# Latent convolution on 32x32 tiles of the array, and layer norm with the channels on the partitions

## The chip, the cores and the metric

The kernel runs on one core of one Trainium2 chip, with the engines TensorE (PE, its weight loads PEld), VectorE (DVE), ScalarE (ACT) and GpSimd (POOL), and with all its transfers issued from SyncE (SP). The metric is the time of one execution on the device in microseconds (us), the median of several runs.

## The reference

One layer with two branches runs over 256 context tokens and 2048 latent tokens (32 rows of 64 columns) of 1024 channels. Cut to what the change touches:

```python
u = (rms_norm(x, g_pre) * (1 + scale) + shift) @ w_in      # -> z, xbc, dt, ga, gb, gsil
y_ssd = rms_norm(ssd_scan_both_ways(...) * silu(z), norm_g)
h = ga * sigmoid(gb)                            # conformer branch, 1024 channels
h = depthwise_conv(h, conv_w, conv_b)           # 31 taps along axis 1 of the grid
h = silu(layer_norm(h, ln_g, ln_b)) * silu(gsil)  # norm over the 1024 channels of a token
out = concat([y_ssd, h]) @ w_out                # (tokens, 2048) @ (2048, 1024)
y = x + gate * rms_norm(out, g_post)
```

For the latent tokens the grid is 32 x 64 and the convolution runs along its 32 rows, so each channel's convolution is a 32x32 banded matrix applied to a 32x64 image.

## The kernel before

The tokens are 18 tiles of 128 (`NT`; two of them context). The projections come first, with float32 split into a high and a low float32r part, so that each product is three matmuls (`mm_cm`, L378 to L380; in the profile `sp`, `xp`, `ga`, `gb` are their PSUM banks). The scan over the tiles (`py`, `po`, `pst`) and the convolutions are woven between them as `extra`, step by step. Last comes the **out stage**, a loop over `order` (the tiles from 17 down to 2, then 1 and 0), from about 1420 us to the end.

The program's order is not only the written one: the tile framework is told to schedule with its own timeline, and it settles in which order each engine takes its instructions. Each engine then works strictly in that order, and waits at an instruction whose inputs are late.

**Latent convolution** (`lat_conv`, eight groups `j` of 128 channels). Channels lie in four row blocks of 32 partitions (a partition is a grid row). Each step `u` of four expands 32 channels' bands from `kd` into a block-diagonal 128x128 operand `kbuf` (four ACT copies a step, L622; two buffers), and eight matmuls (L634, `cp`) take 64 columns of image `x` as stationary operand and `kbuf` as the moving one, with the two 64-column halves of the array. VectorE adds the bias and puts the result into `vt` (L639), and it is stored by token into `CVL`. `ctx_conv` does the context's convolution on VectorE, transposes it (L594) and stores it by token into `CVC`.

**Layer norm and out stage.** For every tile:
- `conf_pre` (L1037): load `cn` by token, statistics with `bn_stats`, `cr` = rstd on GpSimd (`rstd_of`, L135), and `(n - mean) * rstd` in one VectorE pass (L1047).
- `conf_act` (L1050): eight transposes (L1058, `ct`) put channels on the partitions, ScalarE applies `silu` with the channel's scale and bias (L1061) from PSUM, VectorE multiplies with `gsl` (L1063). `conf_hl` splits into `ph` and `pl`.
- `ssd_pre` (L968): `qo` matmuls, `y` of the scan times silu(z), its square, summed over eight blocks (`zr`, L991).
- `ssd_norm` (L1002): one matmul sums `zr` over the partitions (`pm`, L1004), then `yms` and `yr` = rstd. `ssd_scale` (L1010): one matmul spreads `yr` over the partitions (L1012), VectorE scales `y` (L1013); `ssd_hl` splits it into `yh` (ACT, L1019) and `yl` (VectorE, L1020).
- `out_part` (L1073): 96 matmuls of 512 columns (L1078, `op`), 48 with the tile's `yh`/`yl` and 48 with its `ph`/`pl`, into two PSUM banks.
- `finish` (L1081): sums of squares of the two banks on ScalarE (L1087), then scale, add and store.

Of the kernel before, what the change touches and what calls it, by code (L numbers as in the profile page):

```python
# [67 lines left out]
def backbone_kernel(ctx, tc, xa, xt_in, cols, rows, wconv, conf_b, gp_row, bg_row, state0, w_mod, w_dt, w_in, w_out,  # L68
# [19 lines left out]
    CVC = dram("cvc", [NCTX * P, D])  # L88
    CVL = dram("cvl", [LAT, D])
# [437 lines left out]

    def gab_unit(half, j, hb):
        wb = next_w()
        wa = next_w()  # L530
# [72 lines left out]
    def lat_conv(j, lp, kbuf):  # L603
        cbb = lp.tile([P, HD], F32, tag="cbb", name=f"cbb{j}", bufs=2)
        for h in range(2):
            c0 = j * P + h * 64
            DMA.dma_start(cbb[h * 64:(h + 1) * 64], conf_b[c0:c0 + 64].partition_broadcast(64))
        kd = lp.tile([P, 32, 32], F32, tag="kd", name=f"kd{j}", bufs=1)
        for c4 in range(4):
            src = bass.AP(tensor=wconv.tensor, offset=(j * 4 + c4) * 64 * 32, ap=[[32, 32], [1, 1024]])  # L610
# [4 lines left out]
        for c4 in range(4):
            DMA.dma_start(x[c4 * 32:(c4 + 1) * 32], src[c4])

        def expand(u):
            kt = kbuf[u % 2]
            for c4 in range(4):  # L620
                rs = slice(c4 * 32, (c4 + 1) * 32)
                S.copy(kt[rs, :, rs].rearrange("p (h q) r -> p h q r", h=2),  # L622
                       kd[rs].rearrange("p r (h u q) -> p u h q r", h=2, u=4)[:, u])

        vt = lp.tile([P, 32, HD], F32, tag="cvv", name=f"cvv{j}", bufs=1)
        yield
        expand(0)
        yield
        for u in range(4):
            kt = kbuf[u % 2]  # L630
            ps = bank("ss", f"cp{j}_{u}")
            for q in range(4):
                for h in range(2):
                    T.matmul(ps[h * 64:(h + 1) * 64, q * P:(q + 1) * P], x[:, h * 16 + u * 4 + q, :], kt[:, h * 4 + q, :],  # L634
                             start=True, stop=True)
# [3 lines left out]
            V.scalar_tensor_tensor(vt[:, ::-1, u * 16:(u + 1) * 16].rearrange("p r c -> p c r"),  # L639
                                   ps.rearrange("p (c r) -> p c r", r=32), 0.5,  # L640
                                   cbb[:, u * 16:(u + 1) * 16].unsqueeze(2).to_broadcast([P, 16, 32]), MUL, ADD)
# [288 lines left out]
    for u in range(2):  # L930
        G.memset(kbuf[u], 0.0)
# [105 lines left out]
    def conf_pre(i):  # L1037
# [3 lines left out]
        for h in range(2):  # L1041
            V.bn_stats(bs[:, 6 * h:6 * h + 6], n[:, h * 512:(h + 1) * 512])
# [187 lines left out]
```

## Time and profile before

| | |
|---|---|
| median of 3 runs | 1878.53 us (1878.14 to 1878.75) |
| the profiled execution | 1882.2 us, span 1880.5 us |
| mean granted TensorE clock | 0.986 |
| latent stage, 950 to 1360 us | PE busy 392.55 us of 410, clock 0.98 |
| out stage, 1420 to 1880 us | PE busy 449.88 us of 460, clock 0.99 |

The table's execution is the one profiled; the runs of the first line were not profiled. Matmuls are pipelined: the duration of one includes the time until its result has landed, and what it takes of the array is read from the start of the next. In rows of the timeline the columns are start, duration, engine, line, operation, output and inputs, count, and in brackets the idle time ahead of the group and what ended it. In rows by line they are busy time, mean ns of one, idle time before them. `PEclk` is the granted clock as a share of full speed.

### The profile page before, as it was taken

The page shows a single profiled execution, that of the slowest core. Times are in us where ns is not written, and L with a number is a line of the kernel's source. Part 1 is how long each engine was busy: PE and PEld are TensorE (multiplying, and loading weights), DVE is VectorE, ACT ScalarE, POOL GpSimd, SP SyncE. Part 2 cuts the span into 40 slices and gives each one's busy share as a digit, 9 for nine tenths or more (in the row PEclk, how much of TensorE's full clock was granted, in tenths as well). Part 3 has the DMA queues.
Part 4 walks back from the last instruction along what each step waited for, and adds up shares of the span by engine and source line. Part 5 has one row for each costly group of instructions (what it writes and reads, how often), then busy time and mean ns, then how long its engine had stood idle before and what let it go on. Part 6 is the DMA issues. An engine that isn't in the chain of part 4 may idle for free.

```text
span 1880.5 us, 26833 instructions
## 1 busy us (share of the span) xinstructions
PE 1825.6 (97%) x9739; PEld 1504.6 (80%) x9739; DVE 1188.2 (63%) x1699; ACT 839.5 (45%) x1786; POOL 269.0 (14%) x351
## 2 busy tenths in 40 slices
PE   7899999999999999999999899999999999999998
PEld 4788887787887888888877677777887888888887
DVE  2477887776545553577585768655427676766662
ACT  3646424443455441644355666675414232232321
POOL 0002001111111100100001011110013333333220
PEclk9899999999999999999999999999999999999999
DMA  8556575564677754545587897978887655555532
GB/s 302 212 200 198 211 239 179 176 222 155 211 269 225 225 200 169 165 154 188 179 195 215 210 242 194 278 185 234 239 268 239 191 174 173 165 172 173 175 102 78
DMA packets 290400, 375.29 MB, mean 200 GB/s; under 512 B 85206, under 2 KB 187478, under 8 KB 290268
## 3 DMA queue, kind: packets, MB, share of 16 engines
q1 hardware_dynamic: 290268, 373.58, 64.2%
q8 instruction: 77, 1.26, 0.3%
q14 instruction: 55, 0.45, 0.1%
HBM read 243.92 MB, written 129.59 MB: 199 GB/s over the span
## 4 chain that ended last, share of the span: by engine, by line
PE 62%; DMA 5%; ACT 3%; issue 3%; DVE 2%; SPq 2%; POOL 0%; POOLq 0%; DVEq 0%; ACTq 0%
PE op L1078 20%; PE sp L378 6%; PE sp L379 6%; PE sp L380 6%; DMA lb<-lt 3%; PE xp L379 2%; PE xp L378 2%; PE xp L380 2%; PE py L720 2%; PE ga L378 2%; PE ga L380 1%; PE po L727 1%; PE ga L379 1%; PE qo L985 1%; PE gb L378 1%
## 5 line engine op out<-in xcount | busy, mean ns | idle before, releaser
L684 ACT ACTIVATE lb<-lb,WB 128x128 f32<-128x128 f32 x576 | 184.1, 391 | 150.9 <-POOL lb L676 149.0
L378 PE MATMUL sp<-hh,wh 128*128 128x512 f32 (+1 forms) x640 | 239.7, 375 | 2.6 <-DVE sth L550 2.6
L379 PE MATMUL sp<-hl,wh 128*128 128x512 f32 (+1 forms) x640 | 237.0, 370 | 0.0
L380 PE MATMUL sp<-hh,wl 128*128 128x512 f32 (+1 forms) x640 | 236.7, 370 | 0.2 <-DMA wl<-wld 0.2
L676 POOL TENSOR_SCALAR_AFFINE_SELECT lb<-lb 128x512 f32<-128x512 f32 x144 | 108.7, 760 | 749.7 <-ACT el L673 416.1
L378 PE MATMUL xp<-hh,wh 128*128 128x512 f32 (+1 forms) x480 | 179.1, 375 | 6.1 <-ACT wh L353 4.0
L379 PE MATMUL xp<-hl,wh 128*128 128x512 f32 (+1 forms) x480 | 179.1, 373 | 0.2 <-DVE hl L299 0.2
L380 PE MATMUL xp<-hh,wl 128*128 128x512 f32 (+1 forms) x480 | 179.2, 374 | 0.0
L475 DVE SCALAR_TENSOR_TENSOR cva<-raw,cwh,cva 128x1280 f32<-128x1280 f32 (+1 forms) x96 | 142.7, 1495 | 15.5 <-ACT cva L469 13.6
L378 PEld LDWEIGHTS sp<-hh,wh 128*128 128x128 f32 x640 | 121.0, 189 | 24.3 <-DVE sth L550 3.1
L380 PEld LDWEIGHTS sp<-hh,wl 128*128 128x128 f32 x640 | 121.0, 189 | 21.6 <-DMA wl<-wld 0.7
L379 PEld LDWEIGHTS sp<-hl,wh 128*128 128x128 f32 x640 | 121.2, 189 | 20.1 <-issue 0.5
L378 PE MATMUL gb<-hh,wh 128*128 128x512 f32 (+1 forms) x320 | 121.9, 381 | 3.4 <-DVE gth L539 3.4
L378 PE MATMUL ga<-hh,wh 128*128 128x512 f32 (+1 forms) x320 | 120.4, 376 | 2.6 <-ACT gth L536 2.6
L379 PE MATMUL gb<-hl,wh 128*128 128x512 f32 (+1 forms) x320 | 119.3, 373 | 0.0
L380 PE MATMUL gb<-hh,wl 128*128 128x512 f32 (+1 forms) x320 | 119.1, 372 | 0.0
L380 PE MATMUL ga<-hh,wl 128*128 128x512 f32 (+1 forms) x320 | 118.1, 369 | 0.0
L379 PE MATMUL ga<-hl,wh 128*128 128x512 f32 (+1 forms) x320 | 117.9, 369 | 0.0
L590 DVE SCALAR_TENSOR_TENSOR cg<-cg,cv 128x256 f32<-128x256 f32 x240 | 113.3, 497 | 2.5
L550 DVE SCALAR_TENSOR_TENSOR sth<-sth,sp 128x512 f32<-128x512 f32 (+1 forms) x80 | 50.4, 630 | 98.4 <-ACT sth L549 98.4
L378 PEld LDWEIGHTS xp<-hh,wh 128*128 128x128 f32 x480 | 92.0, 192 | 23.0 <-ACT wh L353 4.8
L688 DVE TENSOR_TENSOR lb<-lb,lb 128x512 f32<-128x512 f32 x72 | 51.6, 717 | 85.6 <-ACT lb L684 55.8
(219 smaller groups left out, 3860.8 us busy)
## 6 DMA issues: line engine op xcount, KB each, us to landing
lb<-lt SPq DMA_DIRECT2D x144, 256.0 KB, 4.2
wr<-in_w_in SPq DMA_DIRECT2D x88, 256.0 KB, 4.9
whd<-wh SPq DMA_DIRECT2D x44, 512.0 KB, 3.4
wld<-wl SPq DMA_DIRECT2D x44, 512.0 KB, 4.7
wh<-whd SPq DMA_DIRECT2D x44, 512.0 KB, 5.2
wl<-wld SPq DMA_DIRECT2D x44, 512.0 KB, 5.6
xT<-xb SPq DMA_DIRECT2D x18, 512.0 KB, 5.4
yp<-yg SPq DMA_DIRECT2D x36, 256.0 KB, 4.5
```

Source lines behind the costliest of these rows:

```text
L378: T.matmul(ps[:, :BN], wh[:, k, :], hh[:, k, :], start=(k == 0), stop=False)
L379: T.matmul(ps[:, :BN], wh[:, k, :], hl[:, k, :], start=False, stop=False)
L380: T.matmul(ps[:, :BN], wl[:, k, :], hh[:, k, :], start=False, stop=(k == KT - 1))
L475: V.scalar_tensor_tensor(a[:, :n], raw[:, t:t + n], cwh[:, ct * 5 + t:ct * 5 + t + 1], a[:, :n], MUL, ADD)
L550: V.scalar_tensor_tensor(th, th, 1.0, ps[:, :BN], ADD, MUL)
L590: V.scalar_tensor_tensor(acc, g[:, t:t + 256], cv[:, w0 + t:w0 + t + 1], acc, MUL, ADD)
L676: G.affine_select(E[g, hq, d], E[g, hq, d], pattern=[[0, 4], [sg, P]], compare_op=ALU.is_ge, fill=NEG, base=0, channel_multiplier=-sg)
L684: S.activation(lb[:, h, :], lb[:, h, :], AF.Exp, bias=WB[:, i, c + h:c + h + 1])
L688: V.tensor_tensor(a, a, E[g, hq, 1], ADD)
L720: T.matmul(py[g][j * HD:(j + 1) * HD, q * P:(q + 1) * P], xt[g][:, h * HD:(h + 1) * HD], E[g, hq, 0][:, t, :], start=True, stop=True)
L727: T.matmul(po[g][:, q * P:(q + 1) * P], Sf[g][:, q * P:(q + 1) * P], bc[:, 2 + g, :], start=True, stop=True)
L1078: T.matmul(pso[n], lhs[:, k % 8, :], w[:, n * 512:(n + 1) * 512], start=(k == 0 and m == 0), stop=(k == 15 and m == 2))
```

## The change

**Latent convolution.** Each 32x32 band matrix stays as it is (`kt`, one ACT copy of 128x1024 for a group) and becomes the stationary operand of one 32x32 tile of the array; a channel's 32x64 image is the moving one. A group's 128 channels are dealt out so that channel 32u+4q+a lies in row block a and goes to column block u: 64 matmuls fill two banks, in two runs. The result has channels, not tokens, in order, and is stored by channel into one array `CV`. `ctx_conv` drops its transposes and stores there too. The next group's `kd` and `cx` are loaded one group ahead, if `gab_unit` has stored them (`gl_done`, not shown); the bias is loaded once.

**Layer norm.** A tile of `CV` is loaded with channels on the partitions, so the eight transposes go. The mean over the channels is a sum of eight blocks on VectorE (`sum8`) and one matmul with `ones` (`cm`, L1062), and is subtracted from a tile two ahead (`conf_mean`). Its square (ACT, L1068) and its sum `nq` follow one tile ahead (`conf_square`), and its rstd goes through the same two small matmuls as that of the scan's norm: `norms` (`pm`, two columns, L1018) and `spread` (`pn`, two blocks of one bank, L1029). `zr` is summed with `sum8` too. `cn` has two buffers, `v` still one. `silu` reads SBUF.

```diff
-    CVC = dram("cvc", [NCTX * P, D])
-    CVL = dram("cvl", [LAT, D])
+    CV = dram("cv", [D, NT * P])
...
+        S.mul(o, acc, 0.5)
+        DMA.dma_start(CV[j * P:(j + 1) * P, 0:256], o)
...
+        kd = lp.tile([P, 32, 32], F32, tag="kd", name=f"kd{j}", bufs=2)
+        x = lp.tile([P, 32, 64], F32, tag="cx", name=f"cx{j}", bufs=2)
+        lat_in[j] = kd, x
+        for a in range(4):
+            rs = slice(a * 32, (a + 1) * 32)
+            src = bass.AP(tensor=wconv.tensor, offset=(j * 4 + a) * 64 * 32, ap=[[32, 32], [1, 1024]])
+            DMA.dma_start(kd[rs].rearrange("p r g -> p (r g)"), src)
+            DMA.dma_start(x[rs], GL[j][:, 256:].rearrange("(g a) (r w) -> a r g w", a=4, w=64)[a])
+
+    def lat_conv(j, lp, cbb, more):
+        if j not in lat_in:
+            lat_load(j, lp)
+        kd, x = lat_in.pop(j)
+        yield
+        kt = lp.tile([P, 32, 32], F32, tag="kt", name=f"kt{j}", bufs=1)
+        S.copy(kt[:, :, ::-1].rearrange("p g r -> p r g"), kd)
+        if more(j + 1):
+            lat_load(j + 1, lp)
...
+        vt = lp.tile([P, 32, 64], F32, tag="cvv", name=f"cvv{j}", bufs=1)
         for h in range(2):
...
+            ps = {a: bank("ss", f"cp{j}_{a}") for a in (2 * h, 2 * h + 1)}
+            for q in range(8):
+                for u in range(4):
+                    for a in ps:
+                        rs = slice(a * 32, (a + 1) * 32)
+                        T.matmul(ps[a][u * 32:(u + 1) * 32, q * 64:(q + 1) * 64], kt[rs, u * 8 + q, :], x[rs, u * 8 + q, :],
+                                 start=True, stop=True)
+            yield
+            for a in ps:
+                V.scalar_tensor_tensor(vt[:, a::4, :], ps[a].rearrange("p (c w) -> p c w", w=64), 0.5,
+                                       cbb[:, j, a::4].unsqueeze(2).to_broadcast([P, 8, 64]), MUL, ADD)
+            yield
...
         for u in range(4):
...
+            c0 = j * P + u * 32
+            DMA.dma_start(CV[c0:c0 + 32, 256:].rearrange("c (r w) -> r c w", w=64), vt[u * 32:(u + 1) * 32])
...
+
+    def sum8(out, t, v):
+
+        V.tensor_tensor(t, v[:, 0:4, :], v[:, 4:8, :], ADD)
+        V.tensor_tensor(t[:, 0:2, :], t[:, 0:2, :], t[:, 2:4, :], ADD)
+        V.tensor_tensor(out, t[:, 0, :], t[:, 1, :], ADD)
+        return out
...
-        zr = p1.tile([P, P], F32, tag="zr", name=f"zr{i}", bufs=2)
-        V.tensor_reduce(zr, z.rearrange("p q l -> p l q"), mybir.AxisListType.X, ADD)
+        zr = sum8(p1.tile([P, P], F32, tag="zr", name=f"zr{i}", bufs=2), z[:, 0:4, :], z)
...
+    rows8 = lambda t: t.unsqueeze(1).to_broadcast([P, 8, P])
...
+    def norms(i, yz, nq):
+
         pm = bank("ss", f"pm{i}")
...
+        src = [(c, e, t[1]) for c, e, t in ((0, 4.0 * EPS, yz), (1, EPS, nq)) if t]
+        for c, e, t in src:
+            T.matmul(pm[:, c:c + 1], t, ones[:, 0:1], start=True, stop=True)
+        rs = []
+        for c, e, t in src:
+            ms = p1.tile([P, 1], F32, tag=f"ms{c}", name=f"yms{i}{c}", bufs=2)
+            V.tensor_scalar(ms, pm[:, c:c + 1], 1.0 / D, e, MUL, ADD)
+            rs.append((c, rstd_of(p1, ms, f"yr{i}{c}")))
+        return rs
+
+    def spread(i, rs):
+        pb = bank("ss", f"pn{i}")
+        for c, r in rs:
+            T.matmul(pb[:, c * P:(c + 1) * P], r.to_broadcast([P, P]), ident, start=True, stop=True)
+        return pb
...
+    def conf_load(i):
+        n = p2.tile([P, 8, P], F32, tag="cn", name=f"cn{i}", bufs=2)
+        DMA.dma_start(n, CV[:, i * P:(i + 1) * P].rearrange("(c p) t -> p c t", p=P))
         return n
 
-    def conf_act(i, n):
+    def conf_mean(i, n):
+        t = p2.tile([P, 4, P], F32, tag="cs", name=f"cs{i}", bufs=1)
+        t = sum8(t[:, 0, :], t, n)
+        mean = bank("ss", f"cm{i}")[:, 0:P]
+        T.matmul(mean, ones, t, start=True, stop=True)
+        V.scalar_tensor_tensor(n, rows8(mean), -1.0 / D, n, MUL, ADD)
+        return n
...
+    def conf_square(i, n):
+        v = p2.tile([P, 8, P], F32, tag="v", name=f"v{i}", bufs=1)
+        S.activation(v, n, AF.Square)
+        return v, sum8(p2.tile([P, P], F32, tag="nq", name=f"nq{i}", bufs=2), v[:, 0:4, :], v)
+
+    def conf_act(i, n, v, pb):
...
+        V.tensor_tensor(n, n, rows8(pb[:, P:2 * P]), MUL)
+        for k in range(8):
+            S.activation(v[:, k, :], n[:, k, :], AF.Silu, bias=cv[:, C_LNB + k:C_LNB + k + 1],
+                         scale=cv[:, C_LNG + k:C_LNG + k + 1])
...
     for a, i in enumerate(order):
         last = a + 1 == NT
         nxt = None if last else order[a + 1]
         pt = conf_hl(i, v)
         banks(i)
-        out_part(pso[i], yh, 0, 1)
         if not last:
-            yr = ssd_norm(nxt, yz)
-        out_part(pso[i], yh, 1, 3)
+            v, nq = conf_square(nxt, n)
+        out_part(pso[i], yh, 0, 2)
+        if not last:
+            rs = norms(nxt, yz, (v, nq))
+        y = yz[0]
         if a + 2 < NT:
+            n2 = conf_load(order[a + 2])
             yz = ssd_pre(order[a + 2], order[a + 2] == NCTX - 1)
+        out_part(pso[i], yh, 2, 6)
         if not last:
-            n = conf_pre(nxt)
-        out_part(pso[i], yh, 3, 6)
+            pb = spread(nxt, rs)
+            yhn = ssd_scale(nxt, y, pb)
+        out_part(pso[i], yh, 6, 8)
+        out_part(pso[i], pt, 8, 9)
         if not last:
-            yhn = ssd_scale(nxt, yr)
-        out_part(pso[i], yh, 6, 8)
-        out_part(pso[i], pt, 8, 10)
+            v = conf_act(nxt, n, v, pb)
+        out_part(pso[i], pt, 9, 11)
+        if a + 2 < NT:
+            n = conf_mean(order[a + 2], n2)
         if last:
-            out_part(pso[i], pt, 10, 16, (0,))
-            out_part(pso[i], pt, 10, 16, (1,))
+            out_part(pso[i], pt, 11, 16, (0,))
+            out_part(pso[i], pt, 11, 16, (1,))
         else:
-            v = conf_act(nxt, n)
-            out_part(pso[i], pt, 10, 16)
+            out_part(pso[i], pt, 11, 16)
             yh = yhn
         if i == 1:
```

How this moves instructions on TensorE and VectorE (rows of after carry the line numbers of the changed kernel, as do the lines named in this section). First TensorE in the latent stage, at the first group's first run. Before, eight matmuls (`cp_0` is the bank of step 0) stand between the projection's; `ga` is a bank of the projection:

```order
4287 L379 MATMUL ga_1_4_8687<-hl_7344,wh_1_8346 128x512
4288 L380 MATMUL ga_1_4_8687<-hh_7343,wl_1_8345 128x512
4289 L634 MATMUL cp_0_8691<-kbuf_8337,cx_8634 64x128 x8
4290 L378 MATMUL ga_1_4_8687<-hh_7343,wh_1_8346 128x512
4291 L379 MATMUL ga_1_4_8687<-hl_7344,wh_1_8346 128x512
```

After, the run begins so, and goes on in pairs for 64 matmuls:

```order
4283 L378 MATMUL ga_1_4_8669<-hl_7331,wh_1_8334 128x512
4284 L379 MATMUL ga_1_4_8669<-hh_7330,wl_1_8333 128x512
4285 L634 MATMUL cp_0_8674<-cx_8615,kt_8630 32x64
4286 L634 MATMUL cp_1_8675<-cx_8615,kt_8630 32x64
4287 L634 MATMUL cp_0_8674<-cx_8615,kt_8630 32x64
4288 L634 MATMUL cp_1_8675<-cx_8615,kt_8630 32x64
```

There are 16 such runs where there were 30 with `kbuf`.

TensorE in the out stage. Before, the spread of the scan's norm (`pm<-ident,yr`) for the next tile stands inside the running tile's matmuls with `yh` and `yl`; `op_0` and `op_1` are the tile's banks, `woh` and `wol` the weights' parts:

```order
6442 L1078 MATMUL op_0_14110<-woh_12574,yl_14007 128x512
6443 L1078 MATMUL op_1_14111<-woh_12574,yl_14007 128x512
6444 L1012 MATMUL pm_14118<-ident,yr_14122 128x128
6445 L1078 MATMUL op_0_14110<-woh_12683,yh_14006 128x512
6446 L1078 MATMUL op_1_14111<-woh_12683,yh_14006 128x512
```

24 more with `y` and 36 with `ph` and `pl` follow it before the next tile's first `op` (60 in all). After, the same spread is the first `pn` of a pair, with the mean's `cm` between them. In one tile (`op_0_14763` runs, `op_0_14959` comes next):

```order
7474 L1029 MATMUL pn_14854<-ident,yr_14788 128x128
7475 L1062 MATMUL cm_14908<-cs_14904,ones 128x128
7476 L1029 MATMUL pn_14854<-ident,yr_14792 128x128
7477 L1093 MATMUL op_0_14763<-woh_13729,pl_14760 128x512
7478 L1093 MATMUL op_1_14764<-woh_13729,pl_14760 128x512
7479 L1093 MATMUL op_0_14959<-woh_13065,yh_14858 128x512
7480 L1093 MATMUL op_1_14960<-woh_13065,yh_14858 128x512
7481 L1093 MATMUL op_0_14959<-wol_13064,yh_14858 128x512
7482 L1093 MATMUL op_1_14960<-wol_13064,yh_14858 128x512
7483 L1018 MATMUL pm_14979<-ones,zr_14822 128x1
7484 L992 MATMUL qo_15003<-ct_14992,Sb_13062 128x128 x4
7485 L992 MATMUL qo_15009<-ct_14992,Sb_13063 128x128 x4
```

Two matmuls with `pl` of the running tile follow the pair, then four with the next tile's `yh`, and only then `pm` and `qo`. In the tile ahead of it eight follow, and `pm` and `qo` come before the first with `yh`:

```order
7367 L1029 MATMUL pn_14658<-ident,yr_14596 128x128
7368 L1093 MATMUL op_0_14567<-woh_13723,pl_14564 128x512
7369 L1093 MATMUL op_1_14568<-woh_13723,pl_14564 128x512
7370 L1093 MATMUL op_0_14567<-woh_13729,ph_14563 128x512
7371 L1093 MATMUL op_1_14568<-woh_13729,ph_14563 128x512
7372 L1093 MATMUL op_0_14567<-wol_13728,ph_14563 128x512
7373 L1093 MATMUL op_1_14568<-wol_13728,ph_14563 128x512
7374 L1093 MATMUL op_0_14567<-woh_13729,pl_14564 128x512
7375 L1093 MATMUL op_1_14568<-woh_13729,pl_14564 128x512
7376 L1018 MATMUL pm_14783<-ones,zr_14626 128x1
7377 L992 MATMUL qo_14807<-ct_14796,Sb_13062 128x128 x4
7378 L992 MATMUL qo_14813<-ct_14796,Sb_13063 128x128 x4
```

The last 13 tiles alternate between these two kinds; the tiles of the first kind have 7, 2, 8, 2, 0, 0, 0 matmuls after the pair, those of the second 8, 4, 8, 4, 14, 19. Of the four pairs before them one has five matmuls behind it, and the others have 24 or more. `pm` for both norms (`pmn` with `nq`) stands 22 `op` matmuls ahead of the pair.

VectorE at the same place: before, the scaling of `y` (L1013) stands so, with `yl` from `yh` (ACT) behind it:

```order
1349 L988 TENSOR_TENSOR y_14141<-y_14141,z_14143 128x1024
1350 L1013 TENSOR_TENSOR y_13948<-y_13948,pm_14118 128x1024
1351 L991 TENSOR_REDUCE zr_14162<-z_14143 128x128
1352 L1020 TENSOR_TENSOR yl_14200<-y_13948,yh_14199 128x1024
1353 L1063 SCALAR_TENSOR_TENSOR v_14229<-v_14229,gsl_14227 128x1024
1354 L1042 BN_STATS bs_14363<-cn_14361 128x6 x2
```

After, the mean is subtracted first (L1063), then `y` (L1010) and `cn` (L1074) are scaled, then the running tile's `oms`, and `yl` (L1036):

```order
1497 L1022 TENSOR_SCALAR yms_15178<-pm_15175 128x1
1498 L1022 TENSOR_SCALAR yms_15182<-pm_15175 128x1
1499 L1063 SCALAR_TENSOR_TENSOR cn_15186<-cm_15300,cn_15186 128x1024
1500 L1010 TENSOR_TENSOR y_14997<-y_14997,pn_15246 128x1024
1501 L1074 TENSOR_TENSOR cn_14990<-cn_14990,pn_15246 128x1024
1502 L1103 TENSOR_TENSOR oms_15336<-oms_15336 128x1
1503 L1104 TENSOR_SCALAR oms_15336<-oms_15336 128x1
1504 L1036 TENSOR_TENSOR yl_15251<-y_14997,yh_15250 128x1024
```

More of the change, by code (lines that the diff above doesn't have):

```diff
@@ L526, in xbc_phase @@
             pass
+    gl_done = set()
     def gab_unit(half, j, hb):
@@ L540, in gab_unit @@
             DMA.dma_start(GL[j][:, o:o + BN], th)
+        if half:
+            gl_done.add(j)
     def silu_unit(half, c0, dst, j, hb, order=None):
@@ L928, in backbone_kernel @@
     lp = ph_l.enter_context(tc.tile_pool(name="lp", bufs=1, side="right"))
-    kbuf = [lp.tile([P, 8, P], F32, name=f"kbuf{u}") for u in range(2)]
-    for u in range(2):
-        G.memset(kbuf[u], 0.0)
+    cbb = lp.tile([P, 8, 32], F32, name="cbb")
+    for u in range(4):
+        DMA.dma_start(cbb[u * 32:(u + 1) * 32],
+                      conf_b.rearrange("(j u n) -> u j n", u=4, n=32)[u].partition_broadcast(32))
     blocks = post(1, 5)
     cg = lambda name: lp.tile([P, D], F32, tag="cg", name=name, bufs=2)
-    extra = chain(f for j in range(4) for f in (lat_conv(2 * j, lp, kbuf), ctx_conv(j + 4, cg), lat_conv(2 * j + 1, lp, kbuf)))
+    lat = lambda j: lat_conv(j, lp, cbb, gl_done.__contains__)
+    extra = chain(f for j in range(4) for f in (lat(2 * j), ctx_conv(j + 4, cg), lat(2 * j + 1)))
     sc_ = scan(range(9, NT))
@@ L1035, in load_gg @@
         gg[a] = t
-    def conf_pre(i):
-        n = p2.tile([P, D], F32, tag="cn", name=f"cn{i}", bufs=1)
-        DMA.dma_start(n, CVC[i * P:(i + 1) * P, :] if i < 2 else CVL[(i - 2) * P:(i - 1) * P, :])
-        bs = p2.tile([P, 12], F32, tag="bs", name=f"bs{i}", bufs=2)
-        for h in range(2):
-            V.bn_stats(bs[:, 6 * h:6 * h + 6], n[:, h * 512:(h + 1) * 512])
-        mv = p2.tile([P, 2], F32, tag="mv", name=f"mv{i}", bufs=2)
-        V.bn_aggr(mv, bs)
-        V.tensor_scalar(mv[:, 1:2], mv[:, 1:2], EPS, None, ADD)
-        r = rstd_of(p2, mv[:, 1:2], f"cr{i}")
-        V.tensor_scalar(n, n, mv[:, 0:1], r, SUB, MUL)
-        return n
@@ L1109, in backbone_kernel @@
     wo2 = ph_1.enter_context(tc.tile_pool(name="wo2", bufs=1))
-    gap(wo2, 64)
     run(take(blocks, 5))
@@ L1119, in backbone_kernel @@
     for b in range(2):
-        for n, u in enumerate(last):
+        for m, u in enumerate(last):
             run(take(u, 8))
-            if b == 0 and n == 1:
-                yr = ssd_norm(i, yz)
-            if b == 1 and n == 0:
+            if b == 0 and m == 1:
+                rs = norms(i, yz, None)
+            if b == 1 and m == 0:
+                yh = ssd_scale(i, yz[0], spread(i, rs))
                 ph_b[1].close()
                 p2 = ph_1.enter_context(tc.tile_pool(name="p2", bufs=1))
-                gap(p2, 192)
-                yh = ssd_scale(i, yr)
-                nrm = conf_pre(i)
+                n = conf_mean(i, conf_load(i))
     for u in last:
         run(u)
-    v = conf_act(i, nrm)
+    v, nq = conf_square(i, n)
+    v = conf_act(i, n, v, spread(i, norms(i, None, (v, nq))))
     ph_b[2].close()
@@ L1140, in backbone_kernel @@
     yz = ssd_pre(order[1], False)
+    n = conf_mean(order[1], conf_load(order[1]))
     for a, i in enumerate(order):
```

73 lines of the change are left out of this document (7 added, 66 removed).

## The prediction

> **What bounds the kernel now.** I read the page's head and its chain first, then the two stages that the change touches in the view of windows (length, then busy time of PE, PEld, DVE, ACT and POOL, TensorE's clock, DMA share, GB/s).
>
> ```profile
> span 1880.5 us, 26833 instructions
> PE 1825.6 (97%) x9739; PEld 1504.6 (80%) x9739; DVE 1188.2 (63%) x1699; ACT 839.5 (45%) x1786; POOL 269.0 (14%) x351
> PE 62%; DMA 5%; ACT 3%; issue 3%; DVE 2%; SPq 2%; POOL 0%; POOLq 0%; DVEq 0%; ACTq 0%
> ```
> ```profile
> 950.00:1360.00 410.00, 392.55 (x2330) 308.36 (x2329) 270.05 (x436) 248.40 (x555) 42.55 (x64) 0.98 0.82 221
> 1420.00:1880.00 460.00, 449.88 (x2203) 377.68 (x2201) 302.45 (x355) 137.69 (x279) 137.55 (x116) 0.99 0.53 163
> ```
>
> TensorE bounds both stages. VectorE has slack (66% in each), and the DMA queues do not end the chain. So the change is worth what it takes from TensorE's array, from TensorE's waits and from the half clock behind them, less what it adds of the three. Who waits, then (total, times, longest; then groups by line: busy, mean ns, idle before):
>
> ```profile
> PE cp L634 <- ACT kbuf L622: 10.0, 6, 2.7
> PE op L1078 <- ACT woh L961: 2.2, 1, 2.2
> ```
> ```profile
> L634 PE MATMUL cp<-kbuf,cx 128*64 128x128 f32 x512 | 37.1, 291 | 12.4 <-ACT kbuf L622 10.0 <-DMA cx<-gl 1.9 <-DVE cvv L639 0.3
> L622 ACT COPY kbuf<-kd 32x256 f32<-32x256 f32 x128 | 83.3, 657 | 19.6 <-DMA kd<-in_wconv 11.8 <-PE cp L634 6.0
> ```
>
> The latent matmuls wait 12.4 us in all, 10.0 of it for the expanding copies. Such a wait costs twice, as the windows behind four of them show:
>
> ```profile
> 1040.64 1.25 PE L634 MATMUL cp<-kbuf,cx 128*64 128x128 f32 x10 [2.67 <-ACT kbuf L622]
> 1179.01 1.98 PE L634 MATMUL cp<-kbuf,cx 128*64 128x128 f32 x16 [2.68 <-ACT kbuf L622]
> 1258.93 1.45 PE L634 MATMUL cp<-kbuf,cx 128*64 128x128 f32 x13 [1.91 <-DMA cx<-gl]
> 1445.75 0.73 PE L1078 MATMUL op<-woh,ph 128*128 128x512 f32 x2 [2.20 <-ACT woh L961]
> ```
> ```profile
> 1040.77:1044.18 3.41, 3.41 (x20) 2.80 (x20) 3.41 (x7) 3.31 (x7) 0.78 (x1) 0.50 0.22 66
> 1177.30:1184.13 6.83, 5.12 (x34) 4.69 (x35) 2.92 (x4) 5.79 (x15) 0.63 (x1) 0.50 0.97 287
> 1259.22:1262.63 3.41, 3.41 (x26) 2.26 (x21) 0.61 (x2) 0.88 (x3) 0.63 (x1) 0.50 1.14 259
> 1446.95:1453.78 6.83, 5.89 (x14) 4.63 (x15) 6.83 (x7) 3.17 (x6) 0.00 (x0) 0.50 0.58 184
> ```
>
> After gaps of 1.9 to 2.7 us the granted clock is 0.50 for 3.41 or 6.83 us, so each gap costs at least another 1.7 us. The Trainium skill ("TensorE: Matmul & The Clock Gate", "What's actually happening") puts the fall to half clock behind an idle window of about 3.4 us; these rows show it behind shorter gaps, and the rows decide.
>
> **The change part by part: the latent stage.** A clean run of the old matmuls, between matmuls of the projection (start, duration):
>
> ```profile
> 1234.14 0.40 PE L380 MATMUL sp<-hh,wl 128*128 128x512 f32 x1
> 1234.47 1.09 PE L634 MATMUL cp<-kbuf,cx 128*64 128x128 f32 x16
> 1235.49 0.50 PE L378 MATMUL sp<-hh,wh 128*128 128x512 f32 x1
> 1235.83 0.39 PE L379 MATMUL sp<-hl,wh 128*128 128x512 f32 x1
> ```
> ```profile
> 1618.91 0.62 PE L1078 MATMUL op<-woh,ph 128*128 128x512 f32 x2
> 1619.36 0.62 PE L1078 MATMUL op<-wol,ph 128*128 128x512 f32 x2
> 1619.81 0.62 PE L1078 MATMUL op<-woh,pl 128*128 128x512 f32 x2
> 1620.27 1.03 PE L1058 MATMUL ct<-ident,cn 128*128 128x128 f32 x8
> 1621.06 0.70 PE L1078 MATMUL op<-woh,ph 128*128 128x512 f32 x2
> 1621.60 0.63 PE L1078 MATMUL op<-wol,ph 128*128 128x512 f32 x2
> ```
>
> A 512-column matmul takes 0.2265 us of the array (from 1618.91 to 1619.81 are four). The run then takes 1235.83 - 1234.14 - 2 x 0.2265 = 1.24 us. What a record of it costs alone is read from full-width matmuls of the same 128 columns:
>
> ```profile
> 1608.68 1.95 PE L985 MATMUL qo<-ct,Sb 128*128 128x128 f32 x16
> 1610.38 0.71 PE L1078 MATMUL op<-woh,yh 128*128 128x512 f32 x2
> ```
>
> Sixteen in 1.70 us, 106 ns each. The old run's 16 records on halves of the array can't take that one after the other in 1.24 us: they run two at a time, 16 x 53 ns = 0.85 us, and 0.39 goes on switching shapes. What goes: 512 records x 53 ns = 27 us, 30 runs' switching 11.7, the copies' waits 10.0, and half of the three half-clock windows behind latent waits (13.65 us), 6.8. Together 55.5 us. The copies' 83.3 us of ScalarE become eight copies of 128x1024 (about 1.05 us, by L1019 below); they ran beside TensorE, so beyond the waits this is worth nothing.
>
> What comes: 16 runs of 64 matmuls of 64 columns, 128 records of 53 ns (half of 106) if each runs alone. How many of the eight tiles run at once no row shows for this form. The nearest is the modulation's burst, four column tiles, two records of 256 columns (212 ns) each:
>
> ```profile
> 27.15 0.62 PE L239 MATMUL mp<-wm,sc 128*2 128x256 f32 x8
> ```
>
> One after the other the eight would need 1.7 us; the burst is over in 0.62, so its four column tiles overlap. For a run that gives 6.8 us with no overlap, 3.4 with two tiles at once (as in the old run), 1.7 with four (as here), 0.85 with all eight. I take 1.75: four column tiles are shown side by side, two row blocks nowhere. With 0.39 for switching, 16 x 2.14 = 34 us. Add 3 us for new waits: the first group's loads cannot be ahead, and one such wait was 1.9 us (row at 1258.93). The context's 16 transposes go, 2 us by the row at 1620.27 (eight in about 0.9). So the stage gains 55.5 + 2 - 34 - 3 = about **21 us**; with eight at once 35, with two a loss of 6, with none a loss of 60.
>
> The Trainium skill ("TensorE: Matmul & The Clock Gate", "Wait — 56ns, not 53.3ns?") has starts never closer than about 25 ns, however short the matmul: an estimate of 3.2 us a run, by which the gain of 21 here would be a loss of 2. The row at 27.15 has eight records in 0.62 us that last longer than 25 ns each, and no long run of short ones, so the trace doesn't test it.
>
> **The out stage: what TensorE does less.** From the row at 1619.81 to that at 1621.06 are two `op` matmuls and the eight transposes; 1621.60 shows that the next `op` pair still loses 0.09: 0.88 us in all for the transposes with their switching. In their place stand one more `pm`, one more `pn` and `cm`, each about 0.21 us (106 ns for each of two records). That saves about 0.23 us x 17 = 4 us.
>
> **The out stage: new waits.** Before, TensorE never idles between the steady tiles, whose period is 24.99 us:
>
> ```profile
> 1600.17 0.37 SPq L1052 DMA_DIRECT2D gsl<-gs  x1
> 1625.16 0.37 SPq L1052 DMA_DIRECT2D gsl<-gs  x1
> ```
>
> The spread of the scan's norm stands 60 matmuls, 13.6 us, ahead of the next tile's first `op`. The change ties it to the layer norm's: both `pm` columns share a bank, both rstd come together, and `nq` is late since `v` has one buffer and its square (ScalarE) can start only when the running tile's `pl` has read it. So `pn`, `cm`, `pn` come with 0 to 8 matmuls left. What then lies between them and the next tile's `yh`:
>
> ```profile
> L1013 DVE TENSOR_TENSOR y<-y,pm 128x1024 f32<-128x1024 f32 x18 | 21.8, 1209 | 2.9 <-PE pm L1012 2.9
> L1063 DVE SCALAR_TENSOR_TENSOR v<-v,gsl 128x1024 f32<-128x1024 f32 x18 | 22.0, 1224 | 58.9 <-ACT v L1061 58.9
> L1019 ACT CAST yh<-y 128x1024 fp32r<-128x1024 f32 x18 | 19.0, 1053 | 24.8 <-DVE y L1013 23.9
> L1087 ACT ACTIVATE o<-op 128x512 f32<-128x512 f32 x36 | 21.0, 589 | 23.5 <-PE op L1078 23.5
> L986 DVE TENSOR_TENSOR elb<-elb,qo 128x512 f32<-128x512 f32 x34 | 21.9, 681 | 7.1 <-DMA elb<-el 5.7 <-PE qo L985 1.4
> L1020 DVE TENSOR_TENSOR yl<-y,yh 128x1024 fp32r<-128x1024 f32 x18 | 21.9, 1217 | 3.9 <-ACT yh L1019 3.9
> ```
>
> VectorE subtracts the mean (of L1063's kind, 1.22), scales `y` (1.21), ScalarE casts `yh` (1.05), and three hand-offs take some 0.2: 3.7 us, less 0.2265 for each matmul left. `pm` and `qo` are queued behind the waiting matmul in the first kind of tile, so nothing covers it. For 0 left: 3.7, three times; for 2: 3.2, twice; for 7 or 8: 2.4, twice (ScalarE first has the two squares of L1087, 1.2 us, which start when those matmuls end); the earlier tile with 5: 2.7. Sum 25 us. In the second kind `pm` and `qo` (2.1 us) and 4 to 19 matmuls lie between; the first `yh` waits about 0.5, and then `yl` (1.22) comes behind the scaling of `cn` (1.21) and the two `elb` (0.68 each), 3.8 us against four matmuls with `yh` (0.9) and ScalarE's cast: 1.5 us. Six times 2.0 is 12. Each of the first kind's eight gaps is as long as those that were followed by half clock: seven of eight at 1.7 us are 12 us. The stage loses 25 + 12 + 12 - 4 = **45 us**, between 21 (the first kind's waits alone) and 55 (half clock behind the second kind's too). By the Trainium skill's idle window of about 3.4 us (the section named above) only the three gaps of 3.7 us would be followed by half clock, and 45 would be 38.
>
> What costs nothing: VectorE gets two more passes of 128x1024 a tile and smaller trades (three adds for each reduction), some 3 to 4 us on 66% of 25; it stays under 21 and beside TensorE. The loads of `cn`, now of 1024 pieces, are issued on SP about a tile earlier than they were, among those of `ct`, `y` and `z` for the tile after next, which have a tile's time: nobody waits for them. GpSimd computes the new rstd in place of `cr`.
>
> **Sum.** -21 + 45 = +24; I take off 2 for waits that hide each other, +22: the profiled execution's 1882.2 us becomes 1904, and the median, 3.7 us below that execution, **1900.5 us**.
>
> **Rivals.**
> 1. *The 32x32 tiles win (faster).* All eight tiles run at once: the latent stage gains 35, and the new waits stay at their lower bound of 21, with no half clock: 1878.5 - 14 = 1864. It decides for this side once the latent gain exceeds the out stage's loss. For it: the overlap of column tiles at 27.15. Against: the order leaves 0 to 8 matmuls before `yh`, against 3.7 us of work that cannot start earlier, and gaps of that length were followed by half clock. Chance 0.15.
> 2. *The small matmuls are bound by their issue.* With two at a time the latent stage loses 6 instead of gaining 21, 1927; with none, 60, 1981. For it: no long run in the trace has records closer than 53 ns. Against: the burst at 27.15. Chance 0.17, most of it near 1927.
> 3. *The parts cancel.* Eight at once against 35 in the out stage, or four against its lower bound: 1878.5. Chance 0.07.
>
> My forecast, four at once and waits near 45, has the remaining 0.61.
>
> **The range.** Down to rival 1, 1864. Up to rival 2 with two at once and the out stage at its upper bound, 6 + 55 = 61 over, less the 2: 1938. Outside lie the tail of rival 2 and a better case of rival 1, under 0.2 together. About 0.2% (3.8 us) is what a measurement of this kernel can tell from no change: faster by more 0.15, within it 0.07, slower 0.78.
>
> **What would show it.** In the profile after: waits of `op` for ACT `yh` of 2 to 4 us in every second tile from about the sixth on, and shorter ones for DVE `yl`; windows at 0.50 in the out stage and a mean clock there below 0.99; a tile period of 27 to 28 us. In the latent stage no wait for the copies, and runs of 128 records of about 1.75 us between their neighbours. I am wrong if the out stage's tiles still take 25 us (then the order's pairs do not matter), or if the runs take under 0.9 or over 3 us.

## The result, and the profile after

The changed kernel takes 1926.18 us in the median of 4 runs (1923.96 to 1931.48), the kernel before 1878.64 (1878.14 to 1880.33): a ratio of 1.0256, interval 1.0234 to 1.0277. It is slower, as forecast, but by 47.5 us where 22 were forecast; it lies in the upper part of the range of 1864 to 1938. The two profiled executions differ by 41.8 us (1923.96 against 1882.2); the working below is made against these two.

The head of the page and the chain, after:

```profile
span 1922.2 us, 29767 instructions
PE 1827.7 (95%) x11223; PEld 1506.5 (78%) x11223; DVE 1212.5 (63%) x1807; ACT 797.5 (41%) x1684; POOL 264.2 (14%) x349
PE 73%; DMA 11%; DVE 9%; issue 3%; ACT 3%; SPq 1%; POOL 1%; POOLq 0%; DVEq 0%; ACTq 0%
```

TensorE's busy time is about what it was (1825.6), the span 41.7 us longer, and VectorE has come into the chain with 9% where it had 2%. To place the 41.7 us I take marks that both kernels have. The projection's last matmul starts at 1419.45 us before and at 1407.34 after: 12.1 us are gained up to there. This figure is one pair's, and it is loose. Two of the experiments leave the order on the compute engines as it was up to 1440 us, and there the same matmul starts at 1413.47 us in the kernel before (the late spread) and at 1404.78 in the changed one (the gaps filled). From there on, in the view of windows, first the start of the out stage (to the first `yh` of its third tile), then its steady part (to the first `yh` of the last tile), before:

```profile
1419.45:1479.40 59.95, 56.35 (x275) 46.70 (x274) 48.66 (x53) 26.01 (x45) 22.66 (x17) 0.94 0.76 231
1479.40:1850.70 371.30, 371.30 (x1830) 312.66 (x1829) 246.76 (x291) 107.50 (x225) 113.79 (x97) 1.00 0.52 159
```

and after:

```profile
1407.34:1478.10 70.76, 57.97 (x269) 47.09 (x268) 54.05 (x66) 29.17 (x47) 21.42 (x18) 0.90 0.69 196
1478.10:1892.80 414.70, 385.02 (x1806) 321.49 (x1804) 271.50 (x377) 126.93 (x239) 107.07 (x97) 0.97 0.51 144
```

The start costs 10.8 us more, the steady part 43.4, and the last tile 0.4 less: 53.8 us lost against 12.1 gained. Before, TensorE was busy for all of the steady part at full clock; now it idles for 29.7 us of it (414.70 less 385.02), at a mean clock of 0.97. Whom it waits for there, in the view of waits:

```profile
PE op L1093 <- ACT yh L1035: 20.5, 9, 3.3
PE op L1093 <- DVE yl L1036: 4.7, 2, 2.4
PE op L1093 <- DVE oms L1104: 4.3, 2, 2.1
```

All of it is the scaled `y` of the next tile (the two matmuls put down to `oms` read `yl`, which ends just before that `oms`). One such wait, in the timelines of TensorE, VectorE and ScalarE:

```profile
1584.54 0.38 PE L1029 MATMUL pn<-ident,yr 128*128 128x128 f32 x2
1584.76 0.39 PE L1062 MATMUL cm<-cs,ones 128*128 128x128 f32 x2
1584.99 0.39 PE L1029 MATMUL pn<-ident,yr 128*128 128x128 f32 x2
1585.13 0.71 PE L1093 MATMUL op<-woh,pl 128*128 128x512 f32 x2
1588.67 0.74 PE L1093 MATMUL op<-woh,yh 128*128 128x512 f32 x2 [2.83 <-ACT yh L1035]
```
```profile
1585.19 1.22 DVE L1063 SCALAR_TENSOR_TENSOR cn<-cm,cn 128x1024 f32<-128x1024 f32 x1 [5.34 <-PE cm L1062]
1586.33 1.21 DVE L1010 TENSOR_TENSOR y<-y,pn 128x1024 f32<-128x1024 f32 x1
1587.57 1.04 ACT L1035 CAST yh<-y 128x1024 fp32r<-128x1024 f32 x1 [0.62 <-DVE y L1010]
```

The pair of spreads ends, two matmuls are left, and the mean's subtraction, the scaling and the cast follow one another for 3.5 us. VectorE had been idle for 5.34 us before: it was not short of time, its work came late. How late, and by what, the rows of the next tile's layer norm show, on four engines:

```profile
1570.44 1.06 ACT L1068 ACTIVATE v<-cn 128x1024 f32<-128x1024 f32 x1 [4.12 <-DVE pl L1085]
1573.54 0.28 DVE L972 TENSOR_TENSOR nq<-v 128x128 f32<-128x128 f32 x1
1579.31 0.28 PE L1018 MATMUL pm<-ones,nq 128*128 128x1 f32 x2
1579.87 1.06 POOL L134 TENSOR_TENSOR yr<-yms,nhalf 128x1 f32<-128x1 f32 x2 [15.96 <-DVE yms L1022]
```

The square does wait for `pl`. But its sum `nq` is there at 1573.82, and TensorE, busy with `op` and waiting for nothing, takes `pm` 5.5 us later; rstd is there at 1580.93, and the first `pn` starts 3.6 us later. In each of the seven steady tiles of the first kind (0 to 8 matmuls behind the pair, and the next tile's `yh` right behind them) these two delays come to 4.1 to 9.2 us, more than the wait that follows (2.1 to 3.3). They are the settled order's, not a wait on the chip.

Behind the gap the clock is halved:

```profile
1589.30:1592.70 3.40, 3.40 (x16) 3.21 (x15) 2.33 (x5) 2.65 (x7) 0.72 (x2) 0.50 0.45 153
```

Eight windows of 3.41 us at 0.50 stand in the steady part. A clean run of the new latent matmuls:

```profile
1127.55 0.39 PE L379 MATMUL ga<-hh,wl 128*128 128x512 f32 x1
1127.86 1.48 PE L634 MATMUL cp<-cx,kt 32*32 32x64 f32 x128
1129.27 0.50 PE L377 MATMUL ga<-hh,wh 128*128 128x512 f32 x1
1129.61 0.39 PE L378 MATMUL ga<-hl,wh 128*128 128x512 f32 x1
```

It takes 1129.61 - 1127.55 - 2 x 0.2265 = 1.61 us, with 1.26 us from the first record's start to the last's: 9.9 ns a record. (0.2265 us is what a 512-column matmul takes of the array, as in the prediction.)

### The profile page after: what moved, and what is told of

It reads as the page before. It is cut to its first block, busy times and chain, and to the rows that moved or that the text cites. A ratio compares the mean times of both kernels' runs of the same rounds, so it can differ in the third digit from the quotient of the medians.

```text
span 1922.2 us, 29767 instructions
## 1 busy us (share of the span) xinstructions
PE 1827.7 (95%) x11223; PEld 1506.5 (78%) x11223; DVE 1212.5 (63%) x1807; ACT 797.5 (41%) x1684; POOL 264.2 (14%) x349
## 4 chain that ended last, share of the span: by engine, by line
PE 73%; DMA 11%; DVE 9%; issue 3%; ACT 3%; SPq 1%; POOL 1%; POOLq 0%; DVEq 0%; ACTq 0%
PE op L1093 18%; PE sp L377 7%; PE sp L378 7%; PE sp L379 7%; PE xp L377 4%; PE xp L378 4%; PE xp L379 4%; DMA lb<-lt 4%; PE ga L377 2%; DVE cg L594 2%; PE ga L379 2%; PE ga L378 2%; PE gb L377 2%; PE gb L378 2%; PE gb L379 2%
## 5 line engine op out<-in xcount | busy, mean ns | idle before, releaser
L378 PEld LDWEIGHTS sp<-hl,wh 128*128 128x128 f32 x640 | 121.3, 189 | 19.7
L1093 PE MATMUL op<-woh,yh 128*128 128x512 f32 x288 | 96.1, 412 | 25.1 <-ACT yh L1035 24.9
L377 PEld LDWEIGHTS xp<-hh,wh 128*128 128x128 f32 x480 | 91.8, 191 | 22.4 <-ACT wh L352 4.4
```

What stands on the lines that cost most here:

```text
L377: T.matmul(ps[:, :BN], wh[:, k, :], hh[:, k, :], start=(k == 0), stop=False)
L378: T.matmul(ps[:, :BN], wh[:, k, :], hl[:, k, :], start=False, stop=False)
L1093: T.matmul(pso[n], lhs[:, k % 8, :], w[:, n * 512:(n + 1) * 512], start=(k == 0 and m == 0), stop=(k == 15 and m == 2))
```

## The experiments

Each kernel was timed against the kernel before on its own chip; medians of before there lie between 1879.95 and 1882.16 us, and the ratios are to those.

### Two buffers for `v`

```diff
-        v = p2.tile([P, 8, P], F32, tag="v", name=f"v{i}", bufs=1)
+        v = p2.tile([P, 8, P], F32, tag="v", name=f"v{i}", bufs=2)
```

> The changed kernel with two buffers for v instead of one, nothing else. The square of the next tile then need not wait until pl has read v; in the order pm with nq stands at 12 matmuls into a tile and the pn pair 60 matmuls ahead of the next tile's first yh. Theory A (the pair comes late because v has one buffer, and the waits and the half clock behind them are all of the loss): no wait of op for yh in the steady tiles, period 24.5 to 25.0 us instead of 28, clock 0.99 there, the out stage shorter by 38 to 45 us, the median at 1881 to 1890. Theory B (VectorE's longer chain per tile, not v's buffer, holds the period): the waits move to ph, pl or nq, the period stays above 27 and the median within 10 us of 1926. Theory C (the waits go but the new shapes cost the array itself): no waits and a period above 25.5.

Measured: 1877.12 us, ratio 0.9988 (0.9973 to 1.0004). In the view of windows the start and the steady part:

```profile
1406.70:1478.50 71.80, 59.24 (x267) 47.92 (x266) 52.79 (x67) 30.12 (x48) 23.61 (x18) 0.88 0.72 203
1478.50:1846.00 367.50, 367.50 (x1797) 310.04 (x1797) 263.88 (x377) 126.66 (x239) 121.36 (x97) 1.00 0.57 160
```

No wait is left in the steady part, the clock is full, and the period is 24.75 us against 24.99 before: 0.24 us less, the small matmuls' saving. Theory A holds, and the median is 4 us better than it said: with a second buffer the whole steady loss goes, some 47 us in the profiled executions (414.7 us against 367.5). What the second buffer changes is the square's wait and also the order that the framework settles, in which the pair now stands 60 matmuls ahead. By the rows of the result, much of the lateness was the order's; the two are not separated here, and an order with `pm` and `pn` directly behind their inputs, with one buffer, was not tried. VectorE does the same work, busy 72% of the steady part, so B falls, and C with it. The start of the stage is as slow as in the changed kernel (71.8 us), which is why the whole is a draw with before and not faster.

### The norms apart

The scan's norm gets its own bank for sum and spread and its old place; `v` keeps one buffer (cut):

```diff
     for a, i in enumerate(order):
...
+        out_part(pso[i], yh, 0, 1)
+        if not last:
+            rs = norms(nxt, yz, None)
+            v, nq = conf_square(nxt, n)
+        out_part(pso[i], yh, 1, 3)
...
+        out_part(pso[i], yh, 3, 6)
+        if not last:
+            yhn = ssd_scale(nxt, y, spread(nxt, rs))
+        out_part(pso[i], yh, 6, 8)
+        out_part(pso[i], pt, 8, 9)
+        if not last:
+            v = conf_act(nxt, n, v, spread(nxt, norms(nxt, None, (v, nq))))
```

> The changed kernel with the two norms apart: the scan's norm has its own pm bank with its spread in it and is written where it was before the change, the layer norm's sum and spread come later in another bank; v keeps one buffer. The scan's spread stands 57 or more matmuls ahead of the next tile's yh. Theory A (the loss is that the scan's norm was tied to the late layer norm): as with two buffers for v, waits for yh gone, period 24.5 to 25.2 us, median 1881 to 1890. Theory B (VectorE's chain holds the period, or banks do, of which this takes as many): period above 27, median within 10 us of 1926.

Measured: 1905.25 us, ratio 1.0132 (1.0099 to 1.0165): between the two theories. The waits, without the stage's start:

```profile
PE op L1093 <- DVE pl L1085: 12.8, 6, 2.5
PE op L1093 <- ACT ph L1084: 5.5, 6, 1.1
PE op L1093 <- ACT yh L1035: 3.2, 1, 3.2
```

The waits for `yh` are gone but for one, and the layer norm's own chain, late because its square still waits for the one `v`, now stops TensorE at `pl` and `ph` (here too the order puts its `pm` 1 to 6 us behind `nq`). So the tie carried the lateness to `yh`, and about half of the loss comes back when it is cut, but the rest of the lateness goes with `v`'s one buffer. Theory A was right on the tie and wrong in taking it for the whole. The stage's start is nearly cured:

```profile
1403.93:1465.84 61.91, 55.60 (x262) 46.28 (x261) 50.56 (x62) 25.79 (x39) 22.14 (x17) 0.92 0.71 210
```

61.9 us between the marks that were 59.95 us apart before and 70.76 in the changed kernel.

### The kernel before with a late spread

```diff
         out_part(pso[i], yh, 3, 6)
-        if not last:
-            yhn = ssd_scale(nxt, yr)
...
             v = conf_act(nxt, n)
-            out_part(pso[i], pt, 10, 16)
+            out_part(pso[i], pt, 10, 15)
+            yhn = ssd_scale(nxt, yr)
+            out_part(pso[i], pt, 15, 16)
```

> The kernel before with one line moved: the spread of the scan's norm and the scaling of y are written behind the layer norm's silu, six matmuls ahead of the tile's end, with no other part of the change. In the order the spread then stands 6 matmuls, or four transposes, ahead of the next tile's yh. Theory A (a late spread alone makes the waits): yh (scaling 1.2, cast 1.05, hand-offs) waits about 2.0 us in every second tile and about 0.5 in the others, half clock behind the longer ones: 25 to 35 us more than the kernel before. Theory B (only the change's longer VectorE chain does): within 5 us of before.

Measured, in a single execution: 1906.91 us, 25.8 above before's median there (1881.14). Theory A, though the longer waits are for `yl` and not for `yh`:

```profile
PE op L1078 <- DVE yl L1020: 14.2, 7, 2.0
PE op L1078 <- ACT yh L1019: 5.0, 2, 3.1
```

Seven waits of 2.0 us, one in every second tile, without any of the change's additions to VectorE. A late spread is enough to make a loss of this kind.

### The gaps filled

```diff
+        if len(rs) == 2:
+            for _ in range(10):
+                T.matmul(pm[:, P:2 * P], rs[1][1].to_broadcast([P, P]), ident, start=True, stop=True)
         return pb
```

> The changed kernel with ten more 128-column matmuls (2.1 us a tile, into a bank already read, their result unused) behind each pair of spreads, where TensorE waits for yh. In the order they displace matmuls of the running tile: 0 or 4 of these are left instead of 0 to 14. Theory J (gaps of about 2 us and more bring the half clock, and that costs 17 us beside the 39 us of idle time): the work grows by 34 us, idle falls by 20 to 25 us, and with gaps under 2 us the half clock in the steady tiles goes too: 1910 to 1925, no slower than the changed kernel although it does more. Theory K (half clock comes whatever the gap, or costs nothing since TensorE waits anyway): 1932 to 1945.

Measured: 1923.58 us, ratio 1.0232 (1.0207 to 1.0257), level with the changed kernel's 1926.18. TensorE does some 2.1 us of useless work in each tile, and the time does not grow. The steady part, by the same marks:

```profile
1476.34:1888.32 411.98, 404.02 (x2105) 344.90 (x2104) 267.27 (x379) 129.99 (x246) 102.68 (x97) 1.00 0.52 146
```
```profile
PE op L1097 <- ACT yh L1039: 7.5, 7, 1.1
PE op L1097 <- DVE oms L1108: 0.5, 1, 0.5
```

It takes 412.0 us where it took 414.7, idle time falls from 29.7 to 8.0 us, the longest wait is 1.1 us, and the granted clock is full. Theory J holds: the half clock belongs to the longer gaps, and what it and the idle time cost is what paid for the filling.

### The context's transposes

The kernel before, with

```diff
-        ps = bank("ss", f"cps{j}")
-        for t in range(2):
-            T.transpose(ps[:, t * P:(t + 1) * P], acc[:, t * P:(t + 1) * P], ident)
         o = g[:, 768:1024]
-        S.mul(o, ps[:, :256], 0.5)
+        S.mul(o, acc, 0.5)
```

> The kernel before without the 16 transposes of the context's convolution and without their bank: ScalarE scales the VectorE sum straight from SBUF, and the same bytes go to the same array untransposed (so the context's convolution comes out turned; nothing else is left out). Theory H (the 7 to 8 us that TensorE gained between 370 and 600 us, where the change touches nothing else, come from these transposes and what waited behind them): the waits of ga, gb and sp between 430 and 590 us go (6 us), the half clock at 586 us too, and the median falls by 6 to 10 us. Theory I (it is chance of the order, or of the run): the transposes' own 2 us, the median within 4 us of before.

Measured: 1874.4 us, ratio 0.9972 (0.9961 to 0.9983), 5.7 us less. What TensorE waits for between 420 and 600 us in the kernel before:

```profile
PE ga L378 <- ACT gth L536: 2.6, 2, 1.7
PE sp L378 <- DVE sth L550: 2.6, 1, 2.6
PE gb L378 <- DVE gth L539: 1.2, 2, 0.6
```

In this kernel, as in the changed one, that stretch has no wait at all; a part of it moves ahead, to one wait for `gth` at 370 us (7.0 us here, 4.3 in the changed kernel, 2.2 before). The median falls a little less than theory H said and more than theory I allowed: dropping the 16 transposes, put at 2 us in the prediction, is worth nearly three times that. That ScalarE and VectorE, which empty the projection's banks, were held up behind them is what the releasers suggest.

### The latent matmuls in one bank

On top of `norms_apart`:

```diff
-        for h in range(2):
-            ps = {a: bank("ss", f"cp{j}_{a}") for a in (2 * h, 2 * h + 1)}
+        for h in range(4):
+            ps = {a: bank("ss", f"cp{j}_{a}") for a in (h,)}
```

> norms_apart with the latent convolution in 32 runs of 32 matmuls, one bank and one block of 32 rows at a time (four tiles of the array), instead of 16 runs of 64 in two banks (eight tiles). Theory D (the 9.9 ns between records of the changed kernel is an issue rate): 64 records in 0.63 us, the same 20 us of records in all, 16 more switches of 0.3 to 0.4 (5 to 6 us more), less what the waits for the banks of yg give back (up to 8 us): about as norms_apart. Theory E (tiles set the rate, four of them 53/4 = 13.3 ns a record): 0.85 us a run, 27 us of records, so the latent stage 5 to 12 us longer than with eight tiles unless the waits go.

Measured: 1914.96 us, ratio 1.018 (1.0144 to 1.0216), 9.7 us above `norms_apart` on the same chip. A clean run:

```profile
1073.62 0.39 PE L379 MATMUL ga<-hh,wl 128*128 128x512 f32 x1
1073.93 1.10 PE L634 MATMUL cp<-cx,kt 32*32 32x64 f32 x64
1074.96 0.50 PE L377 MATMUL ga<-hh,wh 128*128 128x512 f32 x1
1075.30 0.39 PE L378 MATMUL ga<-hl,wh 128*128 128x512 f32 x1
```

1.23 us between its neighbours, with 64 records in 0.88 us: 13.8 ns each, what four tiles at the array's rate give (53/4 = 13.3). Theory E: eight tiles are faster, and 32 x 1.23 against 16 x 1.61 is 13.6 us, of which some 3 came back in shorter waits: with one bank at a time `cp` no longer waits for `yg` (4.3 us in `norms_apart`). What sets the 9.9 ns with eight tiles this does not settle, since with four the array is the slower of the two.

### Two ways at the latent stage's new waits, and the best version

First both cures of the out stage together, `norms_apart` with two buffers for `v`:

> norms_apart with two buffers for v as well: the scan's norm on its own early bank, and the layer norm's square free of pl. Theory A (v's one buffer makes the layer norm late, and the tie only carried that to yh; the stage's start costs 13 us because the first tile's norm chain is read behind the projection): no steady waits, period 24.75 us as with v_two_buffers, and of the start's loss about half back, since in the order the scan's spread no longer stands behind the layer norm's there: out stage 452 to 458 us, about 1868 to 1874 where before is 1880. Theory B (bank turnover with seven small banks a tile for five): waits of op or qo for banks, period above 25, no faster than v_two_buffers.

Measured: 1871.33 us, ratio 0.995 (0.9933 to 0.9967): 0.5% faster than the kernel before. Start and steady part:

```profile
1406.90:1471.00 64.10, 56.60 (x268) 46.08 (x267) 52.12 (x67) 26.79 (x39) 22.27 (x18) 0.92 0.71 214
1471.00:1840.00 369.00, 368.76 (x1796) 309.71 (x1795) 283.85 (x377) 129.19 (x246) 111.81 (x97) 1.00 0.57 162
```

The period is 24.85 us, and the start gives back over 6 of its 10.8 us. Then, on top of this, one of the two latent banks taken from the projection's three:

```diff
-            ps = {a: bank("ss", f"cp{j}_{a}") for a in (2 * h, 2 * h + 1)}
+            ps = {a: bank(("ss", "mm")[a % 2], f"cp{j}_{a}") for a in (2 * h, 2 * h + 1)}
```

> apart_and_two with one of the two banks of each latent run taken from the projection's three banks instead of both from the ring of five. Theory F (the latent matmuls' new waits for yg, and those of po, pst and px behind them, come from taking two banks of the ring of five at once): 5 to 9 us less idle time of TensorE between 950 and 1400 us than in apart_and_two (21 us by v_two_buffers), and the median 5 to 10 us lower. Theory G (the waits come from VectorE's queue, which is late with what it releases, whatever the bank): the same idle time, the median within 4 us, or higher if the projection now waits for its bank.

Measured: 1876.42 us, ratio 0.9973 (0.9957 to 0.9988), 5 us slower, with 27.0 us of idle time in the latent stage against 24.3: theory F fails as a cure. The waits of `cp` for `yg` (3.0 us) do go, but `cp` now waits 3.2 us for `sth`, with which VectorE empties the projection's banks. Last, the results taken out by ScalarE:

```diff
-                V.scalar_tensor_tensor(vt[:, a::4, :], ps[a].rearrange("p (c w) -> p c w", w=64), 0.5,
-                                       cbb[:, j, a::4].unsqueeze(2).to_broadcast([P, 8, 64]), MUL, ADD)
+                S.mul(vt[:, a::4, :], ps[a].rearrange("p (c w) -> p c w", w=64), 0.5)
```

> apart_and_two with the latent convolution's results taken out of PSUM by ScalarE instead of VectorE (so without the bias, which is left out), TensorE's order the same. Theory G (the new waits of the latent stage, behind yg, cvv and yo, come from VectorE's queue, which frees the banks late): TensorE's idle time between 940 us and the out stage falls from 24 us to 12 to 17, and the median by 6 to 12 us. Theory L (the waits are of the scan's own chain, which TensorE now reaches sooner, and who empties the banks doesn't matter): idle 21 to 27 us, the median within 4 us of 1871.

Measured: 1874.25 us, ratio 0.9966 (0.9952 to 0.9979), and 25.2 us idle. Theory G fails too: no gain by either way. The idle time stays whichever bank is used and whoever empties it, which is what theory L said of it; its cause, the scan's own chain, is not shown by that.

## Why the prediction was half right

**The sign and the out stage's steady part: right.** Of the prediction's 45 us, 2.7 were for a wait in the stage's start (the pair with five matmuls behind it), so 42.3 for the steady part, which lost 43.4. The two buffers took away the waits, with their period near 28 us, the second kind's `yl` and the windows at 0.50, as the mechanism asks. The size is in part luck: the waits came to 29.7 us of idle time and not 34.3, eight half-clock windows cost 13.6 and not 12, 3.8 us were saved in matmuls and not 4, and some 4 us stood in no term. About 2 of these are the last matmul's latency ahead of each of 13 gaps (0.39 us of duration against 0.2265 of the array), which the trace counts as busy; the rest is not placed. "`nq` is late since `v` has one buffer" is right only of the order: on the chip `nq` was there 1.8 to 5.6 us before its `pm`. The Trainium skill ("TensorE: Matmul & The Clock Gate", "What's actually happening") has the clock fall after an idle window of about 3.4 us; here eight of the steady part's eleven gaps of 2.1 to 3.3 us were followed by it, and none of the gaps of up to 1.1 us in the kernel with filled gaps.

**The step that failed first: the start of the out stage.** Beyond those 2.7 us the prediction let the stage begin as it did before. The order rows of the other first pairs, with 24 or more matmuls behind them, looked like cover. It lost 10.8 us. TensorE waits 3.9 us for `ph` and 1.9 for `pl` of the first tile, whose layer norm is a chain of its own, read behind the projection's last units; then 4.4 for the second tile's `yh` and 2.6 for the third's `nq`, with half clock behind the first and third of these waits. With the norms apart only the wait for `ph` is long (5.7 us), and the start loses 2.0 us: so most of this loss, too, hangs on the tie of the two norms.

**The term that was mis-sized: the latent stage, 21 us.** 12.1 us were gained up to the last projection matmul, and of these 7.5 are there already at 780 us, before any latent matmul; the context's transposes, put at 2, are worth 5.7 in the experiment. What is left to the 32x32 tiles in this pair is 4.6 us. The sum for their array time was too careful: a run costs 1.61 us and not 2.14, so 25.8 us come and not 34, and 12.9 are saved. What failed was "3 us for new waits". The groups that wait in this stage, after:

```profile
PE cp L634 <- DVE yg L759: 6.0, 2, 3.1
PE ga L377 <- DMA wh<-whd: 2.6, 1, 2.6
PE pst L731 <- DVE cvv L638: 2.4, 1, 2.4
PE po L725 <- DVE yg L759: 2.0, 1, 2.0
```

The waits for `kbuf` are gone, as forecast, but TensorE idles 22.4 us between 950 us and the last projection matmul, where it idled 17.7 before (11.9 of it waits that went): 16.6 us of new waits. It stands at half clock for 20.5 us, where it was 17.1. So waits and half clock, priced at 13.8 us of gain, cost 6.4.

How far one pair carries: the kernel with filled gaps, with the changed kernel's order in this stage, idles 17.7 us here, and the kernel before with a late spread, with the order before, 16.6 and is 3.5 us ahead at 780 us with its transposes in place. So new waits of 12 to 17 us are shown, and that the stage gains less than 21 (16 at most, over the five kernels with the same latent matmuls in two banks of the ring of five and both executions of the old order); the division of 12.1 into 7.5 and 4.6 is not. Two ways at the new waits brought nothing. That they are the scan's own chain of VectorE and ScalarE steps, which TensorE now reaches sooner, is argued from the releasers and not shown.

**The sum.** 8.1 for the start (10.8 less the 2.7 that were priced), 8.9 for the latent stage (21 less 12.1), 2 that were taken off for waits that hide each other and weren't found, 1.1 in the steady part, less 0.4 in the last tile: the 19.7 us by which 41.7 exceeds the 22 forecast.

**The rivals.** The first had the gain of 35 from eight tiles at once; eight tiles do run at once, but the gain went into waits, and the out stage's loss was over its bound of 21. The second, issue, is refuted in its size: records start 9.9 ns apart over a run, where it needed 27 to 53. The third, that the parts cancel, fails with a loss of 47.5 us.

## What to carry to other kernels

A buffer count can decide a schedule: before tying two reductions to one pair of matmuls, follow back which of their inputs comes last, and to the buffer it waits for. When the trace is there, see how long each input had been ready when its instruction came: what lies between is the order's, not the chip's. Count the matmuls that the order leaves between a value's last dependence and its first use, tile by tile, and price what exceeds them; then do the same for the first tile, where nothing is ahead. And waits that a change removes are not a gain until it is known what the engine meets next: here the 11.9 us of waits that went came back in full as waits elsewhere.

## What the runs showed of the hardware

Tiles of 32x32 in two row blocks and four column blocks run side by side: 128 records of 64 columns took 1.26 us, where one tile alone would need 6.8 by an estimate (53 ns each, half of the 106 of a 128-column record). In a run the first 32 records start within 0.24 us, 7.5 ns apart, and the other 96 take 1.0 us, 10.7 apart. Eight tiles at the array's rate would give 6.6 (53/8), so something other than the array slows a long run; whether it is the supply of instructions or the weight loads, one to each record, no run here separates. With four tiles (13.8 ns a record against 53/4 = 13.3) the run is bound by the array.

Starts 7.5 to 9.9 ns apart are below the floor of about 25 ns between starts in the Trainium skill ("TensorE: Matmul & The Clock Gate", "Wait — 56ns, not 53.3ns?"), and so are starts of whole matmuls, two records each, at about 20 ns. Here they are starts on different tiles.
